# The second layer's two FFNs: every gate and up column pair as seven block products, two of the weight sums made by accumulating DMA, 1/rms of the up half applied behind the out-projection

## The chip, the core and the metric

The kernel runs on one NeuronCore of a Trainium2 chip, in one launch. The metric is the device time of that launch in microseconds. TensorE (PE) multiplies into PSUM banks; VectorE (DVE), ScalarE (ACT) and GpSimd (POOL) do the elementwise work; transfers are issued from SP, ACT and POOL. DRAM tensors are float32; products are made of float32r halves (a high part, cast by ACT, and a low part, the remainder, made by DVE), three matmuls for one product: high by high, high by low, low by high.

## What is computed

A two-layer decoder trunk over 512 tokens of width 1024. Each layer is `x += 1/2 FFN1; x += mixer; x += 1/2 FFN2`; the mixer of the first layer is an SSD scan, that of the second an S5 state-space model. The part that this change touches is the second layer's FFN, which occurs twice (`f1_1`, `f2_1`):

```python
D_MODEL, SEQ, FFN_DIM = 1024, 512, 2816

def rmsnorm(x, g):
    xf = x.astype(jnp.float32)
    xf = xf * lax.rsqrt(jnp.mean(xf * xf, axis=-1, keepdims=True) + NORM_EPS)
    return xf.astype(x.dtype) * g

def swiglu(h, w_in, w_out):
    gate, up = jnp.split(h @ w_in, 2, axis=-1)
    return (jax.nn.silu(gate) * up) @ w_out

def reference(...):
    for i in range(DEPTH):
        x = x + 0.5 * swiglu(rmsnorm(x, ffn1_norm[i]), ffn1_w_in[i], ffn1_w_out[i])
        ...
        x = x + 0.5 * swiglu(rmsnorm(x, ffn2_norm[i]), ffn2_w_in[i], ffn2_w_out[i])
    return rmsnorm(x, final_norm)
```

## The kernel before

x stays in SBUF, transposed, as eight tiles `xT[d]` of 128 features by 512 tokens. The stages run in the order `f1_0`, `ssd`, `f2_0`, `f1_1`, `s5`, `f2_1`, final norm. 1/rms depends on the token alone, so an FFN multiplies the un-normalised (but gained) x first and scales by `rbc` (1/rms, the same in all partitions) behind the product.

An FFN works in three parts of 8, 7 and 7 column blocks f (`PARTS`). For each f it makes 128 gate columns and 128 up columns over 512 tokens, `silu(gate) * up`, and splits that into `ah`, `al`. At a part's end eight out-projections (one for each d, 24 or 21 matmuls of 512 tokens, L276 to L278) are evicted by DVE into `xT[d]` (L596, one operation: times 0.5 and add).

In `f1_1` and `f2_1` (kind `"wino"`) the blocks alternate between two forms:
- `Plain`: gate and up as two ordinary projections, 8 steps of the inner dimension by three matmuls by 512 tokens each, 48 matmuls.
- `Seven`: the two column blocks (gate, up) by two token halves (`lo`, `hi`, 256 each) with the inner dimension in two halves (even and odd blocks of 128) form a 2 x 2 by 2 x 2 block product, made of seven products instead of eight. Each product is 4 steps by three matmuls of 256 tokens (`prod`, L361), 84 matmuls in all. `run(n)` makes product n and evacuates it; `gate()` ends the gate half and applies `silu`; `out()` ends the up half.

The token-side sums of the seven products (`t1` to `t4`) are made once per FFN, as x arrives, by `Prep.combine` (called from `take(d)` when `xT[d]` is final), into tiles of the pools `hpool` (tags `hH`, `hL`) and `hx` (tags `hx`, six buffers, and `hy`, two). `Prep.square` sums the squares; `compact_sum` (64 tiny matmuls, L155) reduces them over the partitions, `newton_rsqrt` (DVE) makes 1/rms, `bcast` spreads it by four PE transposes.

The weight-side sums of a `Seven` block are made for each f by DVE: `sums` and `sums2`, four 128 x 512 operations, the second two on POOL for the first block of an FFN (`seven_ahead2`). Weights arrive as `wst` tiles (512 KB, four buffers, loaded by SP in `fetch_w`), are cast into `whi` by ACT and made into `wlo` by DVE (three buffers each).

PE's order is that of the program (`manual_schedule(engines=MAN)`) in `f1_1`, `s5` and `f2_1`; the ACT and DVE operations of `seven_in` are held in program order too (`pin`). SP's and POOL's transfers are placed by the scheduler behind the waits that their buffers need. `seven_in` is the order of the in-projections written by hand, with u the current block, n the next, v the previous. `seven_first` makes the first block of parts two and three ready during the out-projections before; `seven_ahead` and `seven_ahead2` do so for the first block of an FFN during the stage before it.

Of the kernel before, what the change touches and what calls it, by code (L numbers as in the profile page):

```python
# [31 lines left out]
def trunk_kernel(ctx, tc, x, ffn1_norm, ffn1_w_in, ffn1_w_out, mix_norm, ffn2_norm, ffn2_w_in, ffn2_w_out,  # L32
# [86 lines left out]

    def late_cols():  # L120
        V.tensor_copy(vrow[2][0:16].rearrange("a (h p) -> a h p", p=64), sdr[:, :, None].to_broadcast([16, 2, 64]))
        for i in range(3):
            cols_of(i)

# [42 lines left out]
    class Prep:  # L167
# [8 lines left out]
        def square(self, d):  # L176
# [7 lines left out]
            elif d < KD - 1:  # L184
                V.tensor_tensor(self.acc, self.acc, sq, op=OP.add)
            else:
                self.ps = compact_sum([self.acc, sq])
# [17 lines left out]
        def finish(self):  # L205
            self.y4 = newton_rsqrt(self.ps[:, 0:4], 4, 1.0 / D)
# [3 lines left out]
        def combine(self, d, g):  # L210
# [6 lines left out]
            S.activation(h, xT[d], AF.Copy, scale=g)  # L217
            self.H[d], self.L[d] = h, l
            m = d % 2 + 1
            self.B[f"{m}1", j], self.B[f"{m}2", j] = (h[:, lo], l[:, lo]), (h[:, hi], l[:, hi])  # L220
            if d % 2 == 0:

                V.scalar_tensor_tensor(l, xT[d], g, h.bitcast(F32), op0=OP.mult, op1=OP.subtract)
                a = self.a = self.tmp("a")
                S.activation(a[:, lo], xT[d][:, lo], AF.Copy, scale=g)
                V.scalar_tensor_tensor(a[:, hi], xT[d][:, hi], g, a[:, lo], op0=OP.mult, op1=OP.subtract)
                if j % 2 == 0:
                    self.v = hx[0].tile([128, 2, T], F32R, name="hy", bufs=2)
                s = slice(j % 2 * 256, j % 2 * 256 + 256)
                S.copy(self.v[:, 0, s], a[:, hi])  # L230
                V.tensor_tensor(self.v[:, 1, s], a[:, hi], self.v[:, 0, s].bitcast(F32), op=OP.subtract)
                self.B["t1", j] = self.v[:, 0, s], self.v[:, 1, s]
                return

            a, b, c = self.a, self.tmp("b"), self.tmp("c")
            V.scalar_tensor_tensor(b[:, lo], xT[d][:, hi], g, a[:, hi], op0=OP.mult, op1=OP.subtract)
            V.tensor_tensor(b[:, hi], b[:, lo], a[:, lo], op=OP.subtract)
            V.scalar_tensor_tensor(c[:, lo], xT[d][:, lo], g, b[:, lo], op0=OP.mult, op1=OP.subtract)
# [42 lines left out]
    class Seven:  # L281


        def __init__(self, pr, w_in, f, fp, pin=lambda i: i):
            self.pr, self.fp, self.pin, self.A = pr, fp, pin, {}
            self.wg, self.wu = [fetch_w(w_in[:, c0:c0 + 128], KD)[0] for c0 in (f * 128, FF + f * 128)]
            self.a = [[self.half(t_, e) for e in range(2)] for t_ in (self.wg, self.wu)]
# [8 lines left out]
        def split(self, st):
            hi = wpool.tile([128, KD, 128], F32R, name="whi", bufs=3)
            hs = [slice(4 * i, 4 * i + 4) for i in range(2)]
            for i in range(2):
                self.pin(S.copy(hi[:, hs[i]], st[i] if type(st) is list else st[:, hs[i]]))  # L300

            def low():
                lo = wpool.tile([128, KD, 128], F32R, name="wlo", bufs=3)
                for a, b in zip(st, hs) if type(st) is list else ((st, slice(0, 8)),):
                    self.pin(V.tensor_tensor(lo[:, b], a, hi[:, b].bitcast(F32), op=OP.subtract))  # L305
                return hi, lo
            return low

        def direct(self):
            low = self.split(self.wg)  # L310

            def end():
                h, l = low()
                self.A["a11"], self.A["a12"] = [(self.half(h, e), self.half(l, e)) for e in range(2)]
            return end

# [1299 lines left out]
```

## Time and profile before

| what | value |
|---|---|
| median of three runs | 2065.02 us (2061.26 to 2065.13) |
| the profiled execution's own time | 2058.34 us |
| its span, first to last instruction | 2056.6 us |
| mean granted TensorE clock | 0.988 |
| busy: PE, DVE, ACT, POOL | 2013.2, 1410.3, 850.5, 93.6 us |
| DMA | 244.42 MB, mean 119 GB/s |

The profile is one execution. Matmuls overlap in the records: one of 512 tokens lasts 390 ns, but the next starts after less, so distances between starts tell the rate, not durations. The same holds in a smaller measure for DVE and ACT. The stage `f1_1` lies at about 1186 to 1515 us of the span, `f2_1` at about 1686 to 2043. A wait belongs to the instruction that was held; its releaser is inferred.

### The profile page before, as it was taken

The numbers are of one execution on the slowest core, as the hardware profiler recorded it, in microseconds if no ns is written. First come the engines' busy times: TensorE is split into PE (matmuls) and PEld (weight loads), VectorE is DVE, ScalarE is ACT, GpSimd is POOL, SyncE is SP. The second block draws the span as 40 slices with busy tenths as digits, with TensorE's granted clock in tenths as the row PEclk, the third lists the DMA queues.
The fourth block names the chain that finished last, engine by engine and source line by source line (L and its number), as shares of the span: only waits on it lengthen the run. The fifth ranks groups of instructions, "written<-read, shape, count | busy, mean of one in ns | idle before, by whom it ended". The sixth has DMA issues, their size and how long they took to land.

```text
span 2056.6 us, 29323 instructions
## 1 busy us (share of the span) xinstructions
PE 2013.2 (98%) x11555; PEld 1703.2 (83%) x11555; DVE 1410.3 (69%) x2390; ACT 850.5 (41%) x1394; POOL 93.6 (5%) x148
## 2 busy tenths in 40 slices
PE   9999999999999999999999999999996999999997
PEld 7888888888878888887788888898885889888896
DVE  6889445788875888568854676575768577556574
ACT  5323233556653564333422443342454444333343
POOL 1000000021110110000000000000011000000000
PEclk9999999999999999999999999999997999999998
DMA  6354543443443325445553323323388124333341
GB/s 184 97 162 161 152 112 85 112 121 100 121 118 93 105 75 151 124 123 156 154 161 92 92 83 113 93 80 109 107 268 257 51 68 118 103 93 94 91 120 55
DMA packets 411529, 244.42 MB, mean 119 GB/s; under 512 B 44952, under 2 KB 396864, under 8 KB 411136
## 3 DMA queue, kind: packets, MB, share of 16 engines
q1 hardware_dynamic: 381968, 203.19, 34.7%
q0 software_dynamic: 7984, 25.46, 3.9%
q10 hardware_dynamic: 21440, 13.91, 2.4%
q8 instruction: 90, 1.47, 0.3%
q14 instruction: 47, 0.39, 0.1%
HBM read 217.74 MB, written 24.25 MB: 118 GB/s over the span
## 4 chain that ended last, share of the span: by engine, by line
PE 88%; DVE 6%; ACT 2%; DMA 2%; issue 1%; SPq 0%; ACTq 0%; DVEq 0%
PE mm L276 24%; PE mm L277 24%; PE mm L278 24%; PE mm L361 11%; DMA wst<-in_s_glu_w_dram 1%; DVE wlo L269 1%; PE aux L836 1%; DVE cv L697 1%; PE aux L778 0%; DMA d_u<-s5u 0%; DMA wst<-in_ffn_w_in_dram 0%; PE aux L1349 0%; PE aux L741 0%; PE aux L829 0%; DVE z L1331 0%
## 5 line engine op out<-in xcount | busy, mean ns | idle before, releaser
L276 PE MATMUL mm<-hH,whi 128*128 128x512 f32 x1416 | 558.1, 394 | 0.6 <-DVE gt L570 0.6
L278 PE MATMUL mm<-hH,wlo 128*128 128x512 f32 x1416 | 552.5, 390 | 0.5 <-DVE wlo L269 0.5
L277 PE MATMUL mm<-hL,whi 128*128 128x512 f32 x1416 | 552.7, 390 | 0.0
L267 ACT CAST whi<-wst 128x1024 fp32r<-128x1024 f32 (+2 forms) x269 | 267.8, 998 | 570.0 <-PE mm L277 431.6
L269 DVE TENSOR_TENSOR wlo<-wst,whi 128x1024 fp32r<-128x1024 f32 (+2 forms) x269 | 310.6, 1156 | 38.2 <-ACT whi L267 36.2
L278 PEld LDWEIGHTS mm<-hH,wlo 128*128 128x128 f32 x1416 | 266.0, 188 | 57.6 <-DVE wlo L269 0.9
L276 PEld LDWEIGHTS mm<-hH,whi 128*128 128x128 f32 x1416 | 266.2, 188 | 56.5 <-issue 2.6
L277 PEld LDWEIGHTS mm<-hL,whi 128*128 128x128 f32 x1416 | 266.3, 188 | 52.7 <-issue 0.6
L277 PE MATMUL mm<-al,whi 128*128 128x512 f32 x704 | 274.5, 390 | 0.0
L278 PE MATMUL mm<-ah,wlo 128*128 128x512 f32 x704 | 274.3, 390 | 0.0
L276 PE MATMUL mm<-ah,whi 128*128 128x512 f32 x704 | 274.1, 390 | 0.0
L596 DVE SCALAR_TENSOR_TENSOR xT<-mm,xT 128x512 f32<-128x512 f32 x96 | 65.9, 689 | 146.1 <-PE mm L278 145.9
L277 PEld LDWEIGHTS mm<-al,whi 128*128 128x128 f32 x704 | 132.2, 188 | 27.5 <-issue 0.6
L276 PEld LDWEIGHTS mm<-ah,whi 128*128 128x128 f32 x704 | 132.2, 188 | 27.5 <-issue 0.4
L278 PEld LDWEIGHTS mm<-ah,wlo 128*128 128x128 f32 x704 | 132.2, 188 | 27.5 <-issue 0.2
L305 DVE TENSOR_TENSOR wlo<-wst,whi 128x1024 fp32r<-128x1024 f32 x88 | 107.6, 1223 | 26.3 <-ACT whi L300 26.3
L300 ACT CAST whi<-wst 128x512 fp32r<-128x512 f32 x176 | 100.3, 621 | 20.6 <-PE mm L277 16.9
L573 DVE TENSOR_TENSOR up<-mm,rbc 128x512 f32<-128x512 f32 x44 | 30.3, 689 | 82.8 <-PE mm L278 82.6
L697 DVE SCALAR_TENSOR_TENSOR cv<-raw,cols,cv 128x512 f32<-128x512 f32 x96 | 80.8, 847 | 7.6 <-ACT cv L695 6.7
L361 PE MATMUL mm<-hH,whi 128*128 128x256 f32 x288 | 82.5, 286 | 0.3 <-ACT up L378 0.2
L361 PE MATMUL mm<-hH,wlo 128*128 128x256 f32 x288 | 82.0, 285 | 0.0
L361 PE MATMUL mm<-hL,whi 128*128 128x256 f32 x288 | 82.0, 285 | 0.0
(403 smaller groups left out, 2893.9 us busy)
## 6 DMA issues: line engine op xcount, KB each, us to landing
wst<-in_ffn_w_in_dram SPq DMA_DIRECT2D x176, 512.0 KB, 4.0
wst<-in_ffn_w_out_dram SPq DMA_DIRECT2D x64, 448.0 KB, 3.7
wst<-in_ssd_in_proj_dram SPq DMA_DIRECT2D x48, 512.0 KB, 3.9
wst<-in_ffn_w_out_dram SPq DMA_DIRECT2D x32, 512.0 KB, 3.8
dec<-d_cs POOLq DMA_DIRECT2D x16, 512.0 KB, 4.3
opP<-d_P SPq DMA_DIRECT2D x16, 512.0 KB, 6.7
wst<-in_s_glu_w_dram POOLq DMA_DIRECT2D x12, 512.0 KB, 5.9
d_t<-p_cs POOLq DMA_DIRECT2D x8, 512.0 KB, 4.5
```

Of the source, the lines that this page charges most:

```text
L267: S.copy(hi, st)
L269: V.tensor_tensor(lo, st, hi.bitcast(F32), op=OP.subtract)
L276: PE.matmul(ps, hi[:, k], H[k], start=first and k == 0, stop=False)
L277: PE.matmul(ps, hi[:, k], L[k], start=False, stop=False)
L278: PE.matmul(ps, lo[:, k], H[k], start=False, stop=last and k == n - 1)
L300: self.pin(S.copy(hi[:, hs[i]], st[i] if type(st) is list else st[:, hs[i]]))
L305: self.pin(V.tensor_tensor(lo[:, b], a, hi[:, b].bitcast(F32), op=OP.subtract))
L361: PE.matmul(ps, w_[:, j], b_, start=nm not in self.open, stop=False, skip_group_check=True)
L573: V.tensor_tensor(up, pu, pr.rbc, op=OP.mult)
L596: V.scalar_tensor_tensor(xT[d], pd, 0.5, xT[d], op0=OP.mult, op1=OP.add)
L697: V.scalar_tensor_tensor(cv, raw[:, 1 + j:T + 1 + j], col("cw", j * 32 + ct), cv, op0=OP.mult, op1=OP.add)
L836: PE.matmul(py[hh * 64:(hh + 1) * 64, s], st["dtx"][:, c, k0:k0 + 64], M[:, hh, s], start=True, stop=True)
```

## The change

Every block f of the second layer's FFNs becomes a `Seven`; `Plain` goes. `seven_in` has a new order: products 1, (4 of the block before), 2, 6, 5, 7, 3 for each block, with the casts and low parts between them, and `gate()` and `out()` of a block in the middle of the next. At a part's end `out0()` starts the first out-projection before the last block's `gate()`, product 4 and `out()`.

The weight sums are chosen differently (`q1` = up-even + up-odd, `q3` = gate-even + up-even, `q2` = q3 + up-odd, `q4` = gate-odd + q2; ge, go, ue, uo below). `q1` and `q3` are made by DMA: SP loads wu, then gate-even a second time into a tile `wx` (256 KB, tag `hy` of the pool `hx`, two buffers), then wg; POOL issues two transfers of 256 KB that add up-odd onto wu's even half and up-even onto `wx`. DVE makes `q2` (`sum2`) and `q4` in place (`sum4`). POOL's two subtractions in `seven_ahead2` go.

On the token side the signs change: `combine` keeps `t1` beside the first operand in one `hH`/`hL` pair for even d, with negated gains (`ng`, two small tiles made in `late_cols`).

1/rms is no longer applied to up. Each out-projection's eviction in these FFNs becomes two DVE operations: the product times 0.5 times `rbc` into a tile `ev`, and the addition to `xT[d]`.

At an FFN's start, `compact_sum` moves behind products 1, 5 and 2 of the first block, the low part of x (`end_x`) and that of q4 follow it, then `newton`; `bcast` comes after product 3. The cast of x moves ahead of the last `hH` cast. The first block uses a separate PSUM bank (`apart`) for the halves of tokens `hi`.

```diff
+            src = [w_in[:, c0:c0 + 128] for c0 in (f * 128, FF + f * 128)]
+            ge, ue, uo = [src[i].rearrange("(j e p) c -> p e j c", e=2, p=128)[:, e] for i, e in ((0, 0), (1, 0), (1, 1))]
+            self.wu = fetch_w(src[1], KD)[0]
+            self.x = hx[0].tile([128, 2, 4, 128], F32, tag="hy", name="wx", bufs=2)
+            nc.sync.dma_start(self.x[:, 0], ge)
+            self.wg = fetch_w(src[0], KD)[0]
+            G.dma_start(self.half(self.wu, 0), uo, accum_op=OP.add)
+            G.dma_start(self.x[:, 0], ue, accum_op=OP.add)
...
+        def sum2(self):
+            self.pin(V.tensor_tensor(self.x[:, 1], self.x[:, 0], self.half(self.wu, 1), op=OP.add))
+
+        def sum4(self):
+            go = self.half(self.wg, 1)
+            self.pin(V.tensor_tensor(go, go, self.x[:, 1], op=OP.add))
...
         def gate(self):
-            pin, rbc, hi = self.pin, self.pr.rbc, slice(256, 512)
-            pin(V.tensor_tensor(self.gt, self.gt, self.q, op=OP.add))
-            pin(V.tensor_tensor(self.gt, self.gt, rbc, op=OP.mult))
+            pin = self.pin
+            for s in (slice(0, 256), slice(256, 512)) if self.q2 is not self.q else (slice(0, 512),):
+                pin(V.tensor_tensor(self.gt[:, s], self.gt[:, s], (self.q2 if s.start else self.q)[:, s], op=OP.add))
+            pin(V.tensor_tensor(self.gt, self.gt, self.pr.rbc, op=OP.mult))
             pin(S.activation(self.gt, self.gt, AF.Silu))
-            pin(V.tensor_tensor(self.up[:, hi], self.up[:, hi], rbc[:, hi], op=OP.mult))
 
         def out(self):
-            pin, lo = self.pin, slice(0, 256)
-            pin(V.tensor_tensor(self.up[:, lo], self.r[:, lo], self.pr.rbc[:, lo], op=OP.mult))
-            pin(V.tensor_tensor(self.up, self.up, self.gt, op=OP.mult))
...
+            pin, lo, hi = self.pin, slice(0, 256), slice(256, 512)
+            pin(V.scalar_tensor_tensor(self.up[:, lo], self.r[:, lo], -1.0, self.gt[:, lo], op0=OP.mult, op1=OP.mult))
+            pin(V.tensor_tensor(self.up[:, hi], self.up[:, hi], self.gt[:, hi], op=OP.mult))
...
+        for f in range(a, b):
+            n = Seven(pr, w_in, f + 1, fp, pin) if f + 1 < b else None
+            u.banks(first and f == a)
+            if first and f == a:
+                u.run(1)
+                u.run(5)
+                u.run(2)
+                pr.sums()
+                pr.end_x()
+                u.split_4()()
+                pr.newton()
+                u.run(6)
+                n.sum2()
+                n.split_g()()
+                u.run(3)
+                pr.bcast()
+                u.run(7)
+                n.sum4()
+                u, v = n, u
+                continue
+            endx = u.split_x()
             u.run(1)
-            if first and f == a:
-                u.run(5)
+            if v:
+                v.gate()
+            endx()
+            if v:
+                v.run(4)
+            end = u.split_u()
+            u.run(2)
             if v:
                 v.out()
...
                 lo = act(v)
...
+            end4 = u.split_4()
+            end()
             if v:
                 lo()
                 pop()
...
+            end4()
             u.run(6)
...
             if n:
+                n.sum2()
+            u.run(5)
             if n:
-                end()
+                n.split_g()()
             u.run(7)
             if n:
...
+                n.sum4()
+            u.run(3)
+            u, v = n, u
+        out0()
+        v.gate()
+        v.run(4)
+        v.out()
+        act(v)()
+        pop()
...
-                    V.scalar_tensor_tensor(xT[d], pd, 0.5, xT[d], op0=OP.mult, op1=OP.add)
+                    if pr.kind == "wino":
+                        ev = fp.tile([128, T], F32, name="ev")
+                        V.scalar_tensor_tensor(ev, pd, 0.5, pr.rbc, op0=OP.mult, op1=OP.mult)
+                        V.tensor_tensor(xT[d], xT[d], ev, op=OP.add)
+                    else:
+                        V.scalar_tensor_tensor(xT[d], pd, 0.5, xT[d], op0=OP.mult, op1=OP.add)
```

## Rows read from the trace of the kernel before

**Rows 1.** The page's first part: busy us of each engine, share of the span, instructions.

```profile
PE 2013.2 (98%) x11555; PEld 1703.2 (83%) x11555; DVE 1410.3 (69%) x2390; ACT 850.5 (41%) x1394; POOL 93.6 (5%) x148
```

**Rows 2.** The table of busy time by stretches: stretch and its length in us, then for PE, weight loads (PEld), DVE, ACT and POOL the busy us and (instructions started), then granted clock, DMA share, GB/s. The first and last row are the starts of the two FFNs, the second is one part's out-projections, the third one part's in-projections.

```profile
1180.00:1213.00 33.00, 30.52 (x229) 26.92 (x228) 27.99 (x53) 15.32 (x30) 2.77 (x2) 0.95 0.22 65
...
1276.00:1320.00 44.00, 44.00 (x198) 36.48 (x197) 18.96 (x23) 9.13 (x11) 0.00 (x0) 1.00 0.25 72
1320.00:1389.00 69.00, 69.00 (x448) 63.25 (x448) 49.69 (x67) 31.07 (x61) 0.00 (x0) 1.00 0.31 91
...
1660.00:1712.00 52.00, 49.94 (x327) 42.97 (x326) 39.66 (x66) 23.21 (x42) 3.88 (x3) 1.00 0.25 71
```

**Rows 3.** The chain that ended last, in order of time, in the first part of `f1_1`: start us, length us, what. A row of 72 is products 1, 2, 6, 5, 7 and 3 of one `Seven` block; between the rows of block products stand the `Plain` block's matmuls and product 4.

```profile
1213.23 8.63 PE mm L361 x72
...
1234.23 8.63 PE mm L361 x72
```

**Rows 4.** Groups of instructions by line, engine and operation: names, shapes, count, busy us, mean ns of one, idle before. The first is product 1's evacuation, one a `Seven` block; the second the first step of the gate in a `Plain` block.

```profile
L373 ACT COPY gt<-mm 128x256 f32<-128x256 f32 x24 | 8.9, 372 | 106.6 <-PE mm L361 106.6
L412 DVE TENSOR_TENSOR gt<-mm,rbc 128x512 f32<-128x512 f32 x20 | 13.8, 689 | 4.2 <-PE mm L278 2.9
```

**Rows 5.** DVE's instructions in order of time in the first part of `f1_1`: start us, us, engine, line, operation, out<-in, shapes [idle before <-releaser].

```profile
1221.90 0.69 DVE L384 TENSOR_TENSOR gt<-gt,mm 128x512 f32<-128x512 f32 x1 [0.80 <-PE mm L361]
1222.62 0.69 DVE L385 TENSOR_TENSOR gt<-gt,rbc 128x512 f32<-128x512 f32 x1
1223.23 0.42 DVE L387 TENSOR_TENSOR up<-up,rbc 128x256 f32<-128x256 f32 x1
...
1227.53 1.22 DVE L305 TENSOR_TENSOR wlo<-wst,whi 128x1024 fp32r<-128x1024 f32 x1
1228.67 0.68 DVE L412 TENSOR_TENSOR gt<-mm,rbc 128x512 f32<-128x512 f32 x1
...
1230.47 0.41 DVE L391 TENSOR_TENSOR up<-mm,rbc 128x256 f32<-128x256 f32 x1
1230.92 0.69 DVE L392 TENSOR_TENSOR up<-up,gt 128x512 f32<-128x512 f32 x1
```

**Rows 6.** PE, ACT and DVE in order of time at a block's start (the first PE row is product 1's first matmul, the second product 2's), and ACT's 1024-wide cast (count, then min/median/max in ns).

```profile
1213.07 0.28 PE L361 MATMUL mm<-hH,whi 128*128 128x256 f32 x1
...
1214.50 0.28 PE L361 MATMUL mm<-hH,whi 128*128 128x256 f32 x1
...
1214.76 0.37 ACT L373 COPY gt<-mm 128x256 f32<-128x256 f32 x1 [4.59 <-PE mm L361]
1215.02 0.62 ACT L427 CAST ah<-up 128x512 fp32r<-128x512 f32 x1
1215.54 1.14 ACT L300 CAST whi<-wst 128x512 fp32r<-128x512 f32 x2
...
1216.72 1.23 DVE L305 TENSOR_TENSOR wlo<-wst,whi 128x1024 fp32r<-128x1024 f32 x1 [0.35 <-ACT whi L300]
...
L267 ACT CAST whi<-wst x7: 1038/1049/1053, 1639.0 to 1670.1; 128x1024 fp32r<-128x1024 f32 x7
```

**Rows 7.** DMA issues: transfer, queue, count, KB each, median us from issue to landing. In order: the weights in a part's in-projections (1320 to 1389); POOL's S5 weights in a calm stretch (1625 to 1670) and in one with DMA share 1.05 (1500 to 1550); one 256 KB transfer from POOL, of the whole page; and POOL's own time for one issue, from its instructions in order of time.

```profile
wst<-in_ffn_w_in_dram SPq DMA_DIRECT2D x10, 512.0 KB, 4.4
...
wst<-in_s_glu_w_dram POOLq DMA_DIRECT2D x5, 512.0 KB, 4.5
...
wst<-in_s_glu_w_dram POOLq DMA_DIRECT2D x7, 512.0 KB, 6.6
...
d_ER<-p_rER POOLq DMA_DIRECT2D x1, 256.0 KB, 2.5
...
1534.68 0.88 POOL L258 DMA_DIRECT2D wst<-in_s_glu_w_dram  x1 [0.32 <-issue]
```

**Rows 8.** The start of `f1_1`: PE's waits between 1150 and 1215 (who for whom: us, times, longest), then DVE and POOL in order of time.

```profile
PE aux L155 <- ACT sq L178: 1.8, 1, 1.8
PE mm L361 <- DVE hy L231: 0.4, 1, 0.4
...
1171.24 0.74 DVE L239 SCALAR_TENSOR_TENSOR hL<-xT,few,hH 128x512 fp32r<-128x512 f32 x1
...
1180.11 1.51 DVE L236 SCALAR_TENSOR_TENSOR tb<-xT,few,ta 128x256 f32<-128x256 f32 x1
1181.54 1.78 DVE L239 SCALAR_TENSOR_TENSOR hL<-xT,few,hH 128x512 fp32r<-128x512 f32 x1
...
1188.98 0.68 DVE L596 SCALAR_TENSOR_TENSOR xT<-mm,xT 128x512 f32<-128x512 f32 x1
...
1181.30 1.47 POOL L328 TENSOR_TENSOR wst<-wst,tx 128x512 f32<-128x512 f32 x1
```

**Rows 9.** The start of `f2_1`: PE's last matmul of product 5 and the square sum behind it, and DVE's last low part, in order of time.

```profile
1689.33 0.28 PE L361 MATMUL mm<-hy,wlo 128*128 128x256 f32 x1
1691.57 0.43 PE L155 MATMUL aux<-ones,sq 128*32 128x1 f32 x32 [1.96 <-ACT sq L178]
...
1690.34 0.75 DVE L239 SCALAR_TENSOR_TENSOR hL<-xT,cols,hH 128x512 fp32r<-128x512 f32 x1
```

**Rows 10.** The chain that ended last, in order of time: S5's start, and the last eviction of the kernel.

```profile
1534.55 5.92 DMA d_u<-s5u
...
2042.83 0.70 DVE xT L596
```

More of the change, by code (lines that the diff above doesn't have):

```diff
@@ L186, in square, with sums @@
             else:
-                self.ps = compact_sum([self.acc, sq])
+                self.sq = sq
+                if self.kind != "wino":
+                    self.sums()
+        def sums(self):
+            self.ps = compact_sum([self.acc, self.sq])
         def take(self, d):
@@ L291, in half, with banks @@
             return t_.rearrange("p (j e) c -> p e j c", e=2)[:, e]
-        def banks(self):
+        def banks(self, apart=False):
             self.r, self.q, self.open = mm_ps(), mm_ps(), set()
[L296 to L300, printed above, removed]
+            self.q2 = aux_ps() if apart else self.q
@@ L306, in low @@
-                return hi, lo
-            return low
[L309 to L315, printed above, removed]
-        def sums(self):
-            if self.fp:
-                self.xx = self.fp.tile([128, 2, 4, 128], F32, name="wx", bufs=1)
-                self.x = [self.xx[:, i] for i in range(2)]
-            else:
-                self.xx, self.x = None, [self.pr.tmp(nm).rearrange("p (j c) -> p j c", j=4) for nm in ("x", "y")]
-            self.pin(V.tensor_tensor(self.x[1], self.a[1][0], self.a[1][1], op=OP.add))
-            self.pin(V.tensor_tensor(self.x[0], self.x[1], self.a[0][0], op=OP.subtract))
@@ L326, in sums2 @@
-        def sums2(self, eng=None):
-            for o, b_ in ((self.a[0][0], self.a[1][0]), (self.a[0][1], self.x[0])):
-                i = (eng or V).tensor_tensor(o, o, b_, op=OP.subtract)
-                if not eng:
-                    self.pin(i)
-        def split_x(self):
-            low = self.split(self.xx.rearrange("p e j c -> p (e j) c") if self.xx else self.x)
-            def end():
-                h, l = low()
-                self.A["s2"], self.A["s1"] = [(h[:, i:i + 4], l[:, i:i + 4]) for i in (0, 4)]
-            return end
@@ L340, in split_s @@
-        def split_s(self):
-            low = self.split(self.wg)
-            def end():
-                h, l = low()
-                self.A["s3"], self.A["s4"] = [(self.half(h, e), self.half(l, e)) for e in range(2)]
-            return end
-        def split_22(self):
-            h, l = [self.fp.tile([128, 4, 128], F32R, name=nm, bufs=1) for nm in ("wh22", "wl22")]
-            self.pin(S.copy(h, self.a[1][1]))
-            self.pin(V.tensor_tensor(l, self.a[1][1], h.bitcast(F32), op=OP.subtract))
-            self.A["a22"] = h, l
+                self.pin(V.tensor_tensor(lo, st, hi.bitcast(F32), op=OP.subtract))
@@ L377, in run @@
                 self.up = self.fp.tile([128, T], F32, name="up")
-                pin(S.copy(self.up[:, hi], q[:, hi]))
+                pin(S.activation(self.up[:, hi], self.q2[:, hi], AF.Copy, scale=-1.0))
             elif n == 7:
-                pin(V.tensor_tensor(self.up[:, hi], self.up[:, hi], r[:, lo], op=OP.add))
+                pin(V.tensor_tensor(self.up[:, hi], self.up[:, hi], r[:, lo], op=OP.subtract))
         def gate(self):
-            pin, rbc, hi = self.pin, self.pr.rbc, slice(256, 512)
@@ L513, in seven_ahead @@
         pr.u = u = Seven(pr, pr.w_in, 0, None, tc.keep_in_program_order)
-        u.sums()
     def seven_ahead2(pr):
         u = pr.u
-        u.direct()()
-        u.split_x()()
-        u.sums2(G)
+        u.split_g()()
+        u.sum2()
+        u.split_u()()
+        u.sum4()
     def split_act(fp, up, AH, AL):
```

154 lines of the change are left out of this document (50 added, 104 removed).

## The prediction

> **What bounds the kernel now.** I read the page's first part first: TensorE (PE) is busy for 98% of the span, DVE for 69% [rows 1]. The table by stretches comes next: inside the in-projections of the two second-layer FFNs PE is busy for 69.00 of 69.00 us at granted clock 1.00 (the upper level, 2.4 GHz), while VectorE (DVE) has 49.69, ScalarE (ACT) 31.07, POOL nothing, and the DMA engines a share of 0.31; in the out-projections DVE has 18.96 of 44 [rows 2]. So in these FFNs the time is the number of matmuls times their spacing, and whatever replaces matmul time must not put DVE, ACT or a DMA in PE's place. Only at the two starts (1180 to 1213 and 1660 to 1712) is PE idle, 2.48 and 2.06 us [rows 2].
>
> The chain gives the spacing. One `Seven` pair and one `Plain` pair repeat every 21.00 us (1213.23 to 1234.23). 72 block matmuls take 8.63 us, so one takes 0.1199; 84 (seven products of 12) take 10.07. The `Plain` pair's 48 matmuls take what is left, 10.93, which is 0.228 each [rows 3]. The counts of the pairs come from their evacuations: 24 `Seven`, 20 `Plain` [rows 4].
>
> **The main term: 20 pairs change form.** 20 x (10.93 - 10.07) = 17.2 us less on PE. The Trainium skill, "TensorE: Matmul & The Clock Gate", section "Back-to-back issue gap", gives N/2.4 + 2.5 ns for one matmul; as an estimate from that page a `Seven` pair would take 9.2 and a `Plain` pair 10.4, and the term would be 23.7. This trace does not agree (120 and 228 ns, not 109 and 216); since it has both forms, the page's 2039.7 gets no chance of its own.
>
> **Does DVE fit into 10.07 us?** It is pipelined, so I use distances between starts: 1.14 for a 1024-wide low part, 0.60 for 512 wide, 0.72 behind its own predecessor's result, 0.45 for 256 wide [rows 5]. Per pair, in program order: gate add 0.72, times 1/rms 0.61, low of x 1.14, up's two halves 0.45 + 0.45, low of wu 1.14, `al` 0.60, low of q4 0.60, `sum2` 0.60, low of wg 1.14, up subtract 0.45, `sum4` 0.60: 8.50, or 84%. DVE doesn't become the bound by volume; by order it could. I walk one steady pair from the start of its product 1 (t = 0; a product is 1.44 long; order 1, previous 4, 2, 6, 5, 7, 3). PE's result reaches ACT 0.26 after the product's end, the next small ACT start is 0.26 on, a 1024-wide cast takes 1.05, and DVE starts 0.04 after it [rows 6].
> - Product 5 ends at 7.19. ACT copies up at 7.45, casts the next pair's wg from 7.71 to 8.76, and DVE makes its low part from 8.80 to 10.03. The next product 1 starts at 10.07 and needs a low part in its third matmul, at 10.31: 0.28 to spare.
> - Behind it on DVE are the up subtract and `sum4` (to 10.99), so the gate add starts 0.92 into the next pair, the low of x ends at 3.4 (product 6 needs it at 4.31), up's halves at 4.29.
> - Product 4 ends at 2.88. Cast of wu 3.14 to 4.19, low part 4.29 to 5.52; product 5 needs it at 5.99: 0.47 to spare.
> - `al`, low of q4 and `sum2` end at about 7.25; DVE is then idle until 8.80.
> ACT's casts and copies come to about 6 of 10.07. No wait is left on PE, but the first margin is thin.
>
> **Do the DMA sums arrive?** SP now issues 1.25 MB a pair (wu, gate-even, wg) and POOL two sums of 256 KB. POOL has no other work there [rows 2], so nothing stands behind them but each other; on SP what queues behind is the next pair's load and the w_out loads of a part's end. wu's buffer (four `wst`, two a pair) is free when the low part of wu two pairs before has ended, at 5.52. A 512 KB load lands 4.4 after its issue [rows 7], at 9.95. `sum2` must start by 8.11 of the next pair, 18.18 on this scale, or low of wg, and with it product 1, is late. The two sums therefore have A = 8.2 us from the first one's issue to the second one's landing. The trace has no accumulating DMA. Below: a 256 KB POOL transfer lands in 2.5. Above: 512 KB on POOL lands in 6.6 in a stretch with saturated DMA; two of them in a row, 13.2. A sum moves 256 KB in, and reads and writes its target, so the calm 512 KB row is nearest, 4.5; the second is issued 0.9 behind the first (POOL is held 0.88 by one) [rows 7]. I take A = 5.5: hidden, with 2.7 to spare. DMA volume (2.1 MB in 21.00 us goes to 3.6 MB, plus the targets' reads) takes the share of 0.31 to 0.55 or 0.65, no bound.
>
> The Trainium skill, "SBUF — State Buffer", "The 'DVE blocks DMA' trap", speaks against this: POOL's descriptors can't be written while DVE runs in a two-port mode. The same page, "Who interferes with whom", gives `tensor_tensor` no such mode, and this loop has little else on DVE. No run here shows it yet. As a mechanism of this kernel: if each sum waited out one 1024-wide DVE instruction (1.22), A would be 7.9 and the total unchanged; if two, 10.4, which is rival 1, and 3% of its chance.
>
> **The starts.** At the first one DVE is late: while POOL ran its two subtractions (the second 1.47 us), two DVE operations took 1.51 and 1.78, where the wider one had taken 0.74 before, and the last eviction started at 1188.98, with PE then waiting 1.8 for the square sum and 0.4 for the last t1 low part [rows 8]. The change takes the subtractions off POOL, makes one 512-wide operation of a 512-wide and a 256-wide one for each even d in `combine` (0.45 less [rows 5]), and moves `compact_sum` behind product 2, most of which needs nothing of the last d. `split_x`'s cast ahead of the last hH on ACT is hidden while ACT waits for the last xT, if the sums have landed; the low of x now sits before product 6 on DVE. I take the idle 2.5 off (bounds 0, and 4.2 if the granted clock, 0.95 there [rows 2], recovers too). At the second start PE ended product 5 at 1689.6 and waited 1.96 for the square; the last low part came at 1691.1 [rows 9], so product 2's last quarter still waits a little: 1.5 off (bounds 0 and 2.0). Against it stands 1/rms: `newton` now begins after the sums, behind two more low parts, while `bcast` on PE is only two products away. I charge 0.5 at each start (0 to 1.5).
>
> **Evictions and the rest.** Each of the 48 evictions becomes two DVE operations: 0.6 more in 4.8 to 5.5 us of matmuls per d, on an engine at 43% [rows 2]; PE covers it, except at the last d of each FFN, where the second operation stands on the path. The end of the chain shows one of 0.70 there [rows 10], so 2 x 0.7 = 1.4 more (if S5's load wait, DMA-bound in the chain [rows 10], covers one, 0.7). Dropping 1/rms from up, the two 8-column scalings at the kernel's start, the spare bank and the tags cost nothing that PE sees.
>
> **Sum.** -17.2 - 2.5 - 1.5 + 1.0 + 1.4 = -18.8. The profiled execution took 2058.34, 1.7 above its span; it would be 2039.5. It stands 6.7 under the median of the three runs shown, 2065.02; with the same difference I predict 2046.2.
>
> **Rivals.**
> 1. *The sums land late (slower).* Each microsecond of A beyond 8.2 stalls DVE at `sum2`, with low of wg, up subtract, `sum4` and the next gate add behind it, and so product 1. The loads of pair f+1 are released in pair f-1, so a stall d comes every second pair: from the third pair of a part, 3 a part, 9 an FFN, 18 in all. At A = 9.2 the gain is gone (18 x 1.04 = 18.8); at the upper bound 13.2 it is 18 x 5.0 = 90, so 2136; at a middle 11, 50 - 18.8, so 2097. For it: no row has an accumulate, and the target must be read too. Against: calm DMA, idle POOL, 2.7 in hand. 17%, with 5% more near no change.
> 2. *The thin order.* If the chain product 5, copy, cast, low part is 0.3 longer than its margin, product 1 waits in each of about 40 pairs: +12, so 2058. For it: 0.28 and 0.47 are less than one instruction. Against: rows 5 and 6 are the same instructions. 13%, 3% of it beyond the 0.2% bound.
> 3. *The starts gain nothing* and both bounds against me hold (+1.5 each): 2052. 5%.
> My own case: 60%, own range 2041 to 2052 (starts at either bound, run spread).
>
> **Numbers.** 0.2% is 4.1 us, about what a measurement of this kernel can tell from no change. Faster: 60 + 10 + 5 = 75%; within: 3 + 5 = 8%; slower: 17%. For 8 in 10 the range goes from 2039 (all starts at their best, 17.2 + 6.2 + a little spread) to 2067, leaving out most of rival 1.
>
> **What would show it.** Right: block matmuls at 0.12 in rows of 84 per pair, the pair's period 10.07, DVE near 84% in the in-projections, no PE wait there; `sum2`'s wait for a DMA under 1 us; no 2 us wait for the square at the starts. Wrong: a period of 10.5 or more with `sum2` released by a DMA (rival 1) or product 1 released by the low part behind the ACT cast (rival 2); DMA share near 1.

## The result, and the profile after

| | before | after |
|---|---|---|
| median of the runs timed together, us | 2064.27 | 2045.08 (2043.46 to 2048.75, 4 runs) |
| ratio, 95% interval | | 0.9912 [0.9894, 0.993] |
| profiled execution: time, span | 2058.34, 2056.6 | 2043.46, 2041.7 |

The kernel is 19.2 us faster by the medians, 2045.08 against a forecast of 2046.2. The profiled executions are only 14.9 apart; both kernels were profiled once more (experiments 1 and 10), and the means of two spans, 2058.5 and 2041.9, are 16.6 apart. In the three later sets of runs beside the experiments the kernel before has medians of 2061.96 to 2062.6 us, so by those the gain is about 17 to 18 us (ratio 0.9917 in experiment 1).

The page's first part and the queue of POOL's transfers (packets, MB, share of 16 engines):

```profile
PE 1996.5 (98%) x12275; PEld 1724.5 (84%) x12275; DVE 1452.9 (71%) x2484; ACT 899.2 (44%) x1374; POOL 198.6 (10%) x232
...
q0 software_dynamic: 54448, 48.53, 13.1%
```

PE is still the bound at 98% [rows 1]. A part's in-projection in the chain, and the windows of the first start and of four pairs (us, each engine's busy time and instructions, granted clock, DMA share, GB/s):

```profile
1312.09 69.11 PE mm L358 x576
```

```profile
core 0: us, PE busy (x) PEld busy (x) DVE busy (x) ACT busy (x) POOL busy (x), PEclk, DMA share, GB/s
1180.00:1213.00 33.00, 32.81 (x306) 31.32 (x306) 30.40 (x60) 19.97 (x33) 5.06 (x4) 1.00 0.57 121
...
1341.22:1381.53 40.31, 40.31 (x337) 40.22 (x336) 33.03 (x48) 23.37 (x36) 8.00 (x7) 1.00 0.82 172
```

The row of 576 is a part of seven pairs without its last product 4. 69.11 / 576 is 0.1200 a matmul, 84 of them 10.08 us, without a break where [rows 3] had a piece of 72 and then a `Plain` pair. DVE has 33.03 of 40.31, 82%. The DMA share is 0.82, well above the forecast. At the first start the 2.48 us of idle PE [rows 2] are down to 0.19, and the clock is 1.00.

One pair on DVE (start, length, line, operation, idle before it):

```profile
1337.03 0.68 DVE L344 TENSOR_TENSOR wx<-wx,wst 128x512 f32<-128x512 f32 x1
1339.39 1.22 DVE L323 TENSOR_TENSOR wlo<-wst,whi 128x1024 fp32r<-128x1024 f32 x1 [1.68 <-ACT whi L320]
1340.53 0.41 DVE L377 TENSOR_TENSOR up<-up,mm 128x256 f32<-128x256 f32 x1
...
1347.11 0.68 DVE L344 TENSOR_TENSOR wx<-wx,wst 128x512 f32<-128x512 f32 x1
```

From `sum2` to `sum2` is 10.08 us, and nearly all of DVE's idle time in it is the 1.68 us ahead of the low of wg (the low part of that weight tile), which waits for the ACT cast: the place that the walk named. The low ends at 1340.61; the third matmul of product 1 starts at about 1340.96, so 0.35 us to spare (forecast 0.28).

The transfers, from a window of 64 us (queue: packets, MB, share of 16 engines; then issues, KB each, us to landing):

```profile
q1 hardware_dynamic: 16387, 8.23, 46.0%
q0 software_dynamic: 6323, 3.14, 40.2%
...
wx<-in_ffn_w_in_dram SPq DMA_DIRECT2D x6, 256.0 KB, 3.1
wx<-in_ffn_w_in_dram POOLq DMA_DIRECT2D x6, 256.0 KB, 6.3
wst<-in_ffn_w_in_dram POOLq DMA_DIRECT2D x5, 256.0 KB, 4.8
```

The accumulates of 256 KB on POOL's queue land 6.3 us (onto `wx`) and 4.8 us (onto wu) after their issue, by the medians; the plain load of the same size on SP's queue takes 3.1. The queue matters more here than the adding: in experiment 5 a plain 256 KB load on POOL's queue lands in 5.3 and the accumulate behind it in 5.8 (medians between 1300 and 1400 us).

### The profile page after: what moved, and what is told of

Its sections match the earlier page's. It is cut to its first block, busy times and chain, and to the rows that moved or that the text cites. A ratio compares the mean times of both kernels' runs of the same rounds, so it can differ in the third digit from the quotient of the medians.

```text
span 2041.7 us, 31329 instructions
## 1 busy us (share of the span) xinstructions
PE 1996.5 (98%) x12275; PEld 1724.5 (84%) x12275; DVE 1452.9 (71%) x2484; ACT 899.2 (44%) x1374; POOL 198.6 (10%) x232
## 4 chain that ended last, share of the span: by engine, by line
PE 92%; DVE 5%; ACT 2%; issue 1%; DMA 0%; SPq 0%; DVEq 0%; ACTq 0%
PE mm L287 22%; PE mm L289 22%; PE mm L288 22%; PE mm L358 21%; PE aux L798 1%; DVE wlo L280 1%; DVE cv L659 1%; PE aux L740 0%; DMA wst<-in_ffn_w_in_dram 0%; PE aux L703 0%; PE aux L159 0%; PE aux L791 0%; DVE z L1293 0%; PE aux L288 0%; PE aux L287 0%
## 5 line engine op out<-in xcount | busy, mean ns | idle before, releaser
L287 PE MATMUL mm<-hH,whi 128*128 128x512 f32 x1096 | 433.2, 395 | 0.7 <-DVE gt L527 0.7
L289 PE MATMUL mm<-hH,wlo 128*128 128x512 f32 x1096 | 428.0, 391 | 0.4 <-DVE wlo L280 0.4
L288 PE MATMUL mm<-hL,whi 128*128 128x512 f32 x1096 | 427.8, 390 | 0.0
L287 PEld LDWEIGHTS mm<-hH,whi 128*128 128x128 f32 x1096 | 206.0, 188 | 45.1 <-issue 2.6
L288 PEld LDWEIGHTS mm<-hL,whi 128*128 128x128 f32 x1096 | 206.2, 188 | 41.9 <-issue 0.6
L358 PE MATMUL mm<-hx,whi 128*128 128x256 f32 x1056 | 196.7, 284 | 0.0
L358 PEld LDWEIGHTS mm<-hx,whi 128*128 128x128 f32 x1056 | 165.5, 192 | 0.5
L358 PE MATMUL mm<-hx,wlo 128*128 128x256 f32 x528 | 149.9, 284 | 0.5 <-DVE wlo L323 0.5
L358 PE MATMUL mm<-hL,whi 128*128 128x256 f32 x520 | 147.4, 283 | 0.9 <-DVE hL L250 0.7
L358 PE MATMUL mm<-hH,wlo 128*128 128x256 f32 x520 | 147.3, 283 | 0.1
L358 PE MATMUL mm<-hH,whi 128*128 128x256 f32 x520 | 147.1, 283 | 0.0
```

What stands on the lines that cost most here:

```text
L287: PE.matmul(ps, hi[:, k], H[k], start=first and k == 0, stop=False)
L288: PE.matmul(ps, hi[:, k], L[k], start=False, stop=False)
L289: PE.matmul(ps, lo[:, k], H[k], start=False, stop=last and k == n - 1)
L358: PE.matmul(ps, w_[:, j], b_, start=nm not in self.open, stop=False, skip_group_check=True)
```

## Experiments

Differences "to the changed kernel" are to its median of 2044.74 in experiment 1.

**1. The changed kernel again.** No edit.

> The changed kernel once more, for the parts of its trace that the forecast's sum doesn't have. The profile of after is 14.9 us shorter than that of before, where its medians lie 19.2 apart: beside the two FFNs it shows 3 us more around the stage between them, 1.1 more at the end and 1.9 us of a lower granted clock at the second start. If these belong to the change, they stand here again and the ratio stays near 0.991; if they are scatter of one execution, some are gone and the profiled execution is 2 to 5 us shorter (2037 to 2040).

2044.74, ratio 0.9917 [0.9903, 0.993], span 2042.1. The granted clock at the second start, first in the first trace of after, then in this one:

```profile
1682.00:1684.00 2.00, 1.50 (x70) 1.22 (x69) 2.00 (x4) 1.06 (x4) 0.00 (x0) 1.00 0.06 7
1684.00:1686.00 2.00, 2.00 (x12) 2.00 (x12) 1.72 (x11) 0.10 (x1) 0.00 (x0) 0.54 0.44 130
1686.00:1688.00 2.00, 2.00 (x13) 2.00 (x12) 1.87 (x5) 1.22 (x2) 0.65 (x1) 0.61 0.94 268
```

```profile
1682.00:1684.00 2.00, 1.25 (x40) 0.92 (x40) 2.00 (x5) 1.79 (x5) 0.00 (x0) 1.00 1.03 129
1684.00:1686.00 2.00, 1.50 (x59) 1.28 (x49) 1.99 (x4) 0.72 (x2) 0.00 (x0) 1.00 0.01 1
1686.00:1688.00 2.00, 2.00 (x19) 2.00 (x18) 1.67 (x11) 1.13 (x2) 0.00 (x0) 1.00 0.68 191
```

The same kernel, with the same two PE waits (0.7 and 0.5 us), fell to the lower level in one execution and kept 1.00 in the other. The fall is scatter of one execution, not part of the change. Without the fall the profiled execution is no shorter (2043.84 for 2043.46), so my expectation of 2 to 5 us failed. S5 is as long as in the first trace of after (see experiment 10).

**2. Both sums on DVE.**

```diff
-            nc.sync.dma_start(self.x[:, 0], ge)
-            G.dma_start(self.half(self.wu, 0), uo, accum_op=OP.add)
-            G.dma_start(self.x[:, 0], ue, accum_op=OP.add)
...
+            self.pin(V.tensor_tensor(self.x[:, 0], ge, ue, op=OP.add))
             self.pin(V.tensor_tensor(self.x[:, 1], self.x[:, 0], uo, op=OP.add))
+            self.pin(V.tensor_tensor(ue, ue, uo, op=OP.add))
```

> The two sums by accumulating DMA, and the separate load of the gate's even blocks, are undone: only wu and wg are loaded, and DVE makes x0 = ge + ue and ue += uo beside sum2, two 128x512 operations more (0.6 us each by the spacing of such operations in the trace). Theory (the pair's length is its 84 matmuls, DVE idles 1.68 us a pair right behind sum2): 1.2 us fit into the idle, the pair stays at 10.08 us, DVE goes from 82% to 94%, the DMA share of the in-projections falls from 0.82 to about 0.5, and the total is within 3 us of the changed kernel's. Rival (DVE is the bound without the DMA sums): low of wg comes 0.2 to 0.5 us later than its 0.35 us of margin allows, 38 pairs get longer by that, and the total is 8 to 20 us longer. Second rival (the DMA sums cost time that is not seen in waits): 3 us or more shorter.

2046.72, ratio 0.9928 [0.9914, 0.9941]: 2.0 above the changed kernel, inside the run spread. Four pairs:

```profile
1330.00:1370.30 40.30, 40.30 (x338) 40.30 (x337) 38.27 (x57) 23.70 (x36) 0.00 (x0) 1.00 0.37 106
```

The pairs stay at 10.08 us with DVE at 95% and the DMA share at 0.37. The theory holds: the idle in front of the low of wg takes both sums. The first start shows PE waits of 0.4, 0.5 and 0.7 us instead of the 0.2, most of the 2 us. So the accumulating DMAs, the part with the largest risk in the forecast, bring about nothing in the steady pairs.

**3. 1/rms back on the up half**, the evictions one operation again.

```diff
+            pin(V.tensor_tensor(self.up[:, 256:], self.up[:, 256:], self.pr.rbc[:, 256:], op=OP.mult))
...
-            pin(V.scalar_tensor_tensor(self.up[:, lo], self.r[:, lo], -1.0, self.gt[:, lo], op0=OP.mult, op1=OP.mult))
-            pin(V.tensor_tensor(self.up[:, hi], self.up[:, hi], self.gt[:, hi], op=OP.mult))
+            pin(V.scalar_tensor_tensor(self.up[:, lo], self.r[:, lo], -1.0, self.pr.rbc[:, lo], op0=OP.mult, op1=OP.mult))
+            pin(V.tensor_tensor(self.up, self.up, self.gt, op=OP.mult))
```

> 1/rms goes back from the evictions of the out-projection to the up half: one 256-wide operation more and one 512-wide instead of a 256-wide one in each pair on DVE (0.45 + 0.15 us, from 82% to 88% of a pair), and each eviction one operation again. Theory: both fit between DVE's other work, so the pairs stay at 10.08 us, and the second operation at the last d of each FFN, 0.7 us each in the forecast and 0.9 and 1.8 in the trace of after, is given back: 1.4 to 2.7 us shorter than the changed kernel. Rival (thin order): al, the low of q4, sum2 and up's halves come 0.6 later; the low of wu has 0.47 to product 5 and product 5 waits 0.1 to 0.2 us a pair: 4 to 8 us longer. For the second rival, bcast must now be done before the first up is scaled, which both FFNs have long done by then: nothing.

2044.78, ratio 0.9915: no change. Both effects are there and cancel. The pairs go from 10.08 to 10.12, and from the first `sum2` of the first FFN's loop to the last it is 283.48 us against 281.70 (1.8 an FFN). Against that, PE's wait for the last square at the kernel's end, after and here:

```profile
2028.76 0.42 PE L159 MATMUL aux<-ones,sq 128*32 128x1 f32 x22 [1.90 <-ACT sq L182]
```

```profile
2029.41 0.25 PE L159 MATMUL aux<-ones,sq 128*32 128x1 f32 x9 [0.70 <-ACT sq L182]
```

1.2 us back there (1.6 from the sum of the first seven squares to the end of the span), and 0.7 at the first FFN's end (1.81 to 1.08).

**4. The square sum and `newton` early.**

```diff
             else:
                 self.sq = sq
-                if self.kind != "wino":
-                    self.sums()
+                self.sums()
...
-            if self.kind == "wino":
-                return
             self.newton()
```

(and `pr.sums()`, `pr.newton()` gone from the first block)

> The square sum on PE and newton go back to where they stood: the sum right behind the last square, ahead of the first products, newton behind it. Theory: PE waits for the square again at both starts, 2.5 us at the first and 1.5 at the second, less the 0.7 + 0.5 that it waits there now, so 2.5 to 4 us longer than the changed kernel; if the granted clock at the second start then doesn't fall, 1.9 less than that. Rival (the start lost its idle by the combine that issues less on DVE and by POOL without its subtractions, not by the moved sum): no wait comes back and the total is the same.

2049.8, ratio 0.9941: 5.1 longer, so moving both is worth 5 us, more than I gave it, and by another way. PE doesn't wait for the square but for the low of x. PE's waits at the first start, and DVE there:

```profile
PE mm L355 <- DVE wlo L320: 3.2, 1, 3.2
```

```profile
1193.53 0.16 DVE L143 TENSOR_SCALAR nw_v<-aux 128x4 f32<-128x4 f32 x1 [1.12 <-PE aux L159]
...
1195.78 0.16 DVE L150 SCALAR_TENSOR_TENSOR nw_y<-nw_a,nw_y 128x4 f32<-128x4 f32 x1
1195.86 1.22 DVE L320 TENSOR_TENSOR wlo<-wx,whi 128x1024 fp32r<-128x1024 f32 x1
```

`newton` idles 1.12 us for the sum and runs 2.3 us in 13 tiny operations, with the low of x queued behind it; product 6 waits 3.2 us at each start, where the changed kernel waits 0.2 and 1.2 in all. With 0.2 more for hL at the second start that is 6.6 - 1.4 = 5.2. This sum isn't all: the granted clock fell behind both waits in this trace (to 0.62 in 1198 to 1202, 0.51 in 1694 to 1696), each start took 13.28 us from product 1 to `bcast` (8.54 and 11.26 in after), and the profiled execution is 8 us longer than those of the changed kernel. That the listed waits meet the 5.1 of the medians is partly chance.

**5 and 6. The sum of ge and ue later.** The ge block is loaded once more (5), twice more (6) on POOL before the sum.

```diff
             G.dma_start(self.half(self.wu, 0), uo, accum_op=OP.add)
+            for _ in range(n):
+                G.dma_start(self.x[:, 0], ge)
             G.dma_start(self.x[:, 0], ue, accum_op=OP.add)
```

> In each pair the block of the gate's even rows is loaded a second time, on POOL's queue, before the sum is added onto it, so that the sum of ge and ue lands later by one 256 KB transfer, 2.5 to 5 us. The result is the same; nothing else moves. By the trace of after the sum lands 3.3 us before sum2 reads it, and DVE idles 1.68 us behind sum2: 5.0 us of slack. Theory (both DMA sums are hidden with this slack): at most a few sum2 waits in the profile, the pair stays at 10.08 us, the total within 3 us of the changed kernel's. Rival (the forecast's own account, 2.7 us to spare between the second landing and sum2 and no more): 0 to 2.3 us in each pair or each second one, 18 to 38 times: up to 40 to 90 us longer.

> The same with two further loads: the sum of ge and ue lands 5 to 10 us later than in the changed kernel. The result is the same. Theory: the 5.0 us of slack are used up, DVE waits at sum2 for the DMA, the low of wg and with it the next product 1 are late by 0 to 5 us in each pair, so the pair's period goes to 10.1 to 15 us; the total is longer by 38 times what the period gains. By the forecast's rival 1 a delay comes in each second pair only, since a pair's loads are released in the pair before: 18 times. Which of the two it is, the period's list tells. Rival (the loads start earlier than the release of their buffers lets one think): still hidden.

5: 2072.1, ratio to before 1.0044 [1.0028, 1.006]. 6: 2169.89, 1.0521 [1.0505, 1.0537]. PE's waits (us in total, times, longest), 5 and then 6:

```profile
PE mm L360 <- DVE wlo L325: 19.2, 17, 3.1
```

```profile
PE mm L360 <- DVE wlo L325: 88.3, 19, 5.5
```

and `sum2` of three pairs on DVE in 6:

```profile
1367.06 0.69 DVE L346 TENSOR_TENSOR wx<-wx,wst 128x512 f32<-128x512 f32 x1
1384.16 0.69 DVE L346 TENSOR_TENSOR wx<-wx,wst 128x512 f32<-128x512 f32 x1 [6.85 <-DMA wx<-in_ffn_w_in_dram]
1394.46 0.69 DVE L346 TENSOR_TENSOR wx<-wx,wst 128x512 f32<-128x512 f32 x1
```

In 6 the stall comes in every second pair, 19 times: 17.1 us, then 10.3. This is rival 1's account, and the theory of "each pair" in my expectation fell. In 5 it is less regular: DVE waits for the sum at 26 `sum2`, PE 17 times, and pairs take 9.6 to 14.8 us. One pair of 5 gives an estimate of the slack:

```profile
1342.78 1.26 POOL L307 DMA_DIRECT2D wx<-in_ffn_w_in_dram  x1 [0.74 <-DMA wx<-in_ffn_w_in_dram]
...
1349.07 0.69 DVE L346 TENSOR_TENSOR wx<-wx,wst 128x512 f32<-128x512 f32 x1 [3.72 <-DMA wx<-in_ffn_w_in_dram]
```

The added load was issued at 1336.23, so the sum behind it (1342.78) came 6.55 us later; DVE waited 3.72 at `sum2`, so the sum had some 2.8 us in hand there, and the pair took 11.94, 1.86 more than 10.08, so DVE's idle swallowed another 1.86. The trace of after gives 3.3 + 1.68 directly. So PE has about 5 us of slack to this sum, and one transfer of 256 KB more is enough to make the change a loss. My expectation of "within 3 us" for 5 failed: the added load put off the sum by 3.6 to 7.4 us from pair to pair (from its issue to that of the sum), not 2.5 to 5. It also slowed other traffic (512 KB on SP landed in 6.2 us instead of 4.7), and no run separates the two.

In 6 the total is 125 longer, but the waits sum to 88. Most of the rest is the clock behind the long waits, as behind this one:

```profile
1378.00:1384.00 6.00, 3.33 (x28) 3.12 (x27) 0.00 (x0) 1.32 (x2) 2.09 (x3) 1.00 1.10 241
1384.00:1386.00 2.00, 0.00 (x0) 0.00 (x0) 1.84 (x3) 0.98 (x1) 0.68 (x1) 0.55 0.81 118
1386.00:1388.00 2.00, 1.95 (x9) 1.96 (x10) 1.97 (x4) 0.07 (x1) 0.10 (x1) 0.50 0.45 131
1388.00:1390.00 2.00, 2.00 (x11) 2.00 (x11) 1.39 (x2) 0.91 (x2) 0.99 (x1) 0.50 0.01 4
```

About 6 us at the lower level (0.50 of 2.4 GHz). (125 - 88) / 19 is some 1.9 us more for each stall. In 5 most stalls are shorter, and 1320 to 1384 is at 1.00; behind its longest waits, 3.1 and 2.6 us, the clock fell there too (0.66 in 1220 to 1230, 0.83 in 1470 to 1480).

**7. A later cast.** ACT copies up three times.

```diff
-                pin(S.activation(self.up[:, hi], self.q2[:, hi], AF.Copy, scale=-1.0))
+                for _ in range(3):
+                    pin(S.activation(self.up[:, hi], self.q2[:, hi], AF.Copy, scale=-1.0))
```

> ACT copies the up half of product 5 out of its bank three times in place of once, ahead of the cast of the next pair's wg; the result is the same. Two 256-wide copies are 0.6 to 0.75 us, by which the cast of wg and its low part come later. Theory (the chain product 5, copy, cast of wg, low of wg, third matmul of product 1 has 0.28 us to spare by the forecast and 0.35 by the trace of after): product 1 waits 0.25 to 0.45 us in each of about 38 pairs, the total is 10 to 17 us longer, and DVE's other work hides nothing of it. Rival (PE runs ahead far enough, or the scheduler finds another order): no wait, the same time.

2068.87, ratio to before 1.0033: 24 longer than the changed kernel, not 10 to 17. The pair goes from 10.08 to 10.72; 37 x 0.64 = 23.7. The place is the one expected, PE before the third matmul of product 1:

```profile
1325.56 0.28 PE L358 MATMUL mm<-hH,whi 128*128 128x256 f32 x1
1325.68 0.28 PE L358 MATMUL mm<-hL,whi 128*128 128x256 f32 x1
1326.22 0.39 PE L358 MATMUL mm<-hH,wlo 128*128 128x256 f32 x1 [0.27 <-DVE wlo L323]
1326.44 0.28 PE L358 MATMUL mm<-hH,whi 128*128 128x256 f32 x1
```

The list of waits sums to 37 x 0.27 = 10.0 us, yet the wait shown, listed as 0.27, costs more: the start comes 0.54 behind the last one instead of 0.12 (0.42 lost), the next is 0.22 behind (0.10), and product 3 before it starts in the same broken way (0.13): 0.65. The two copies delay the cast by 0.83, so the margin of this chain is 0.83 - 0.42 = 0.41 us. The thin order of rival 2 is real: a delay of the cast by 0.83 us turns the gain into a loss.

**8. Fill the start.** For the last d, `hL` ahead of `c`; the sum over the first seven squares ahead of product 2's last quarter.

```diff
+            if d == KD - 1:
+                V.scalar_tensor_tensor(l, xT[d], g, h.bitcast(F32), op0=OP.mult, op1=OP.subtract)
             V.scalar_tensor_tensor(c[:, lo], xT[d][:, lo], ng_, b[:, lo], op0=OP.mult, op1=OP.subtract)
...
+                if mid and j == KD // 2 - 1:
+                    mid()
```

> At the starts two things move: for the last d, DVE makes the low part hL right behind the two halves of b, ahead of c, so that it comes 0.4 us earlier; and the 16 one-column matmuls over the sum of the first seven squares run inside product 2, ahead of its last quarter, which is the quarter that waits for hL (0.7 us in the trace of after). Theory: that wait goes, 0.4 to 0.7 us; if the granted clock at the second start stays up, which fell there to 0.54 for 4 us behind two short waits and the square sum's matmuls, 1.9 us more: 0.5 to 2.6 us shorter than the changed kernel. Rival: the low of x, 0.5 us behind, becomes the only wait and takes what the first gave, the clock falls the same: within 0.3 us.

2046.9, ratio 0.9922 [0.9907, 0.9937]: no gain; 2.2 longer than the changed kernel by the medians, inside the spread of its runs (2043.55 to 2049.06). At the second start the wait for hL fell from 0.74 to 0.18 and the one for the low of x rose from 0.50 to 0.78; the clock fell here (0.56). The rival's mechanism holds.

**9. Experiments 2 and 3 together.**

> Both edits at once: the two sums on DVE and 1/rms on the up half. Alone, the first left the pair at 10.08 us and the second made it 10.12. By the spacings DVE then has 8.5 + 1.2 + 0.6 = 10.3 us a pair for 10.08 us of matmuls. Theory (there is room for 1.5 us on DVE and no more): DVE sets the period, 10.3 to 10.5, with PE waiting for low parts in each pair and DVE at 97% or more: 8 to 20 us longer than the changed kernel. Rival (spacings overlap better than they add): the period stays within 0.1 of 10.12 and the total within 5 us.

2051.43, ratio 0.9952 [0.9937, 0.9967]: 6.7 longer than the changed kernel. The period is 10.27 (1342.75 to 1353.02), about the 10.3 that the spacings give; the total is a little under the 8 to 20 expected. A stretch of 9, and one of the same length of 3 (four pairs):

```profile
1334.00:1374.48 40.48, 40.48 (x333) 39.92 (x332) 39.79 (x60) 22.53 (x36) 0.00 (x0) 1.00 0.35 101
```

```profile
1328.00:1368.48 40.48, 40.48 (x338) 40.48 (x337) 35.56 (x53) 23.77 (x36) 10.20 (x8) 1.00 0.89 183
```

DVE is at 98% and sets the period. PE shows as busy throughout and no wait is listed here: a matmul lasts 0.28 us in the records, so starts up to 0.28 apart leave no idle. The starts tell: in each pair product 1's third matmul, which needs the low of wg, and the one behind it start 0.21 and 0.23 behind their predecessors (1340.96 and 1341.19) instead of 0.12, which makes up the 0.19 by which the period grew.

**10. The kernel before again.** No edit.

> The kernel before once more, for a second trace of it. In its first trace S5, from its first matmul to product 1 of the second FFN, took 139.3 us, and the FFN's end to S5's first matmul 5.3; in five traces of kernels with the change they are 140.4 to 142.7 and 5.2 to 6.2. If S5 and the granted clock at the second start belong to scatter, this trace has other values than 139.3 and may show the clock fall too (there it stayed up); if the change lengthens S5, it shows 139 to 140 again.

2063.03, span 2060.4. The granted clock at its second start fell to 0.70 and 0.50 where the first trace kept 1.00, so before has this scatter too. From S5's first matmul (L1304 here) to product 1 of the second FFN:

```profile
1548.32 0.69 PE L1304 MATMUL aux<-rm,qsel 128*128 128x64 f32 x2 [2.87 <-DVE rm L1301]
...
1688.81 0.39 PE L361 MATMUL mm<-hH,whi 128*128 128x256 f32 x1
```

140.5 us, after 139.3 in the first trace. In after:

```profile
1535.27 0.69 PE L1266 MATMUL aux<-rm,qsel 128*128 128x64 f32 x2 [3.21 <-DVE rm L1263]
...
1676.67 0.28 PE L358 MATMUL mm<-hH,whi 128*128 128x256 f32 x1
```

141.4, and 141.7 in experiment 1; the kernels of 2, 3, 4, 7, 8 and 9 have 140.4 to 142.7. By the means S5 is some 1.6 us longer with the change, but the ranges touch (140.4 the shortest with it, 140.5 the longer of the two before), and this trace did not show 139 to 140 again. Whether the change lengthens S5, and by what, stays open.

## Why the prediction was right, point by point

Two traces of each kernel, by stretches (means, us):

| stretch | measured | forecast |
|---|---|---|
| product 1 of the first FFN to S5's first matmul: 361.6 to 349.7 | -11.8 | -8.6 - 2.5 + 0.5 + 0.7 = -9.9 |
| S5: 139.9 to 141.6 | +1.6 | 0 |
| product 1 of the second FFN to the end: 370.9 to 364.4 | -6.5 | -8.6 - 1.5 + 0.5 + 0.7 = -8.9 |
| all | -16.6 | -18.8 |

- **Main term, -17.2.** Right: 0.1200 a matmul, 10.08 a pair; the row of 69.11 us for 576 stands in each part of seven. The three experiments that lengthen the pair (6, 7, 9) name what holds it there.
- **DVE fits.** Right in volume (82% for 84%), in order (the idle lies where the walk put it), and in the margin (0.35 by the trace, 0.41 by experiment 7, for 0.28). The second margin, 0.47 at product 5, is confirmed from one side: 0.6 us more on DVE cost 0.04 a pair (experiment 3).
- **The sums arrive.** The outcome was right, the working wrong in three terms. A, the time from the first sum's issue to the second's landing, was 7.6 us and not 5.5: the second lands in 4.8 (the first in 6.3), not 4.5, and is issued 2.8 behind the first, not 0.9, since POOL is held 1.27 by the first and then stands idle 1.2 to 1.6 (in two of five cases the trace names wu's load as what it waits for). The deadline was put on the wrong transfer: `sum2` needs only the sum of ge and ue, which is issued first; the other lands 8.0 to 8.6 us ahead of the cast of wu that reads it. The order helped too: gate-even is loaded 2 us ahead of wu, so the first sum was issued 6.8 to 7.5 us after a product 1's start where the walk had 9.95. And the DMA share was 0.82 against 0.55 to 0.65, since an accumulated MB costs the engines 40.2 / 3.14 = 12.8% of the window where a loaded one costs 46.0 / 8.23 = 5.6%. The queue isn't the reason: in 5's window of 64 us POOL's queue moved 4.17 MB, of which ten accumulates make 2.6, in 41.9%; with those at 12.8% a MB its plain loads come to some 5.4, as on SP (an estimate). The slack to PE came out near 5 us where I gave 2.7, with errors of both signs. Rival 1's mechanism is shown by experiment 6 (19 stalls for its 18); its price by stalls alone is too low where the clock falls.
- **The Trainium skill, "SBUF — State Buffer", "The 'DVE blocks DMA' trap",** says that POOL can't write a transfer's descriptors while DVE runs in a two-port mode. Here POOL's issue of an accumulate took 1.27 us beside a DVE at 82%, and the accumulates landed in 4.4 to 7.9; no transfer stopped. How much of that is descriptor writing beside DVE, no run here separates.
- **The starts.** From product 1's first matmul to `bcast` (PE, start and length), the first start before and after, then the second before and in experiment 1, both at granted clock 1.00:

```profile
1186.30 0.28 PE L361 MATMUL mm<-hH,whi 128*128 128x256 f32 x1
1198.84 0.60 PE L164 MATMUL aux<-ident,nw_y 128*128 128x128 f32 x4
...
1185.93 0.28 PE L358 MATMUL mm<-hH,whi 128*128 128x256 f32 x1
1194.47 0.62 PE L168 MATMUL aux<-ident,nw_y 128*128 128x128 f32 x4
...
1686.47 0.39 PE L361 MATMUL mm<-hH,whi 128*128 128x256 f32 x1
1696.51 0.60 PE L164 MATMUL aux<-ident,nw_y 128*128 128x128 f32 x4
...
1678.32 0.28 PE L358 MATMUL mm<-hH,whi 128*128 128x256 f32 x1
1688.29 0.65 PE L168 MATMUL aux<-ident,nw_y 128*128 128x128 f32 x4
```

The first went from 12.54 to 8.54 (12.65 to 8.55 in the second traces): 4.0 gained, near the upper bound of 4.2 and not the net 2.0 of the sum, since idle and clock both came back. The second went only from 10.04 to 9.97 (from 11.52 to 11.26 where the clock fell): 0.1 to 0.3 for the net 1.0. Two waits of 0.74 and 0.50 stand in the place of one of 1.96, and the sum of the first seven squares, some 0.36 us, which before ran ahead of product 1 there, now lies inside this distance. Of the 0.5 charged for `newton` at each start hardly any was needed (PE's weight load waits 0.2 for it at the second start of experiment 1), and the reason for the gain was mis-stated: experiment 4 shows that `newton` no longer stands in front of the low of x on DVE. What POOL's subtractions and the shorter `combine` gave at the first start, no run isolates.
- **The evictions, +1.4.** The mechanism was right and the size low: from the first FFN's last matmul to S5's first one 6.2 and 7.0 us against 5.3 and 5.1, and from the last matmul to the end of the span 1.8 us more (1.2 of it PE's wait for the square): 3.2 in all. That 1/rms left the pairs was costed at nothing; by experiment 3 it was worth 0.04 a pair and more at the part starts, 1.8 an FFN, which pays for the evictions.
- **S5, 0.** 1.6 us longer by the means, which two traces of before don't settle. The stage wasn't walked.

The terms that failed have both signs (-2.0 at the first start and +0.8 at the second, +1.8 for the evictions, +1.6 in S5), so the total agrees better than they do. With them the first stretch comes to -11.2 and the second to -7.0, where -11.8 and -6.5 were measured; the rest stays open. The nearness of 2046.2 to 2045.08 is luck in part as well: it stands on a median before of 2065.02, and the later medians before are near 2062.

No version beat the changed kernel measurably. Experiment 2 is its equal within the runs' spread, with less traffic.

## What to carry to other kernels

When PE sets the period, walk one period of each helper engine in order and find where its idle time lies: here it took two more operations for nothing on DVE (experiment 2), while 0.83 us on ACT at the wrong place cost the whole gain (experiment 7). For a transfer, ask which consumer needs it first and count from its own landing time; the slack then includes the consumer's idle behind it. Read the period from starts, not from the list of waits.

## What the runs showed of the hardware

- An accumulating DMA of 256 KB landed 4.8 to 6.3 us after issue (medians) beside a DMA share of 0.82, about as a plain load on the same queue (5.3 in experiment 5), but took 2.3 times the DMA engines' time per MB (12.8% against 5.6% of 64 us); POOL was held 1.27 us to issue it, 0.78 for the plain one.
- A PE wait listed as 0.27 us cost 0.52 in starts of matmuls: matmuls of 256 columns are 0.28 long and 0.12 apart, so the start came 0.54 behind the one before and the next 0.22. Starts up to 0.28 apart aren't listed as waits at all, and cost 0.19 a pair in experiment 9.
- Behind stalls of about 5 us the granted clock was at 0.50 to 0.55 for some 6 us; at the second start the same kernel with the same waits of 0.7 and 0.5 us fell to the lower level in one execution and not in another.
